# Where the matmul inputs of a transformer layer lie in on-chip memory, relative to their weights

## The chip, the core and the metric

The kernel runs on one core of a Trainium2 chip. The metric is the device time of one execution in microseconds (us), lower is better. A core has five engines that run their own instruction streams in order: PE (TensorE, matmuls, with its weight loads PEld), DVE (VectorE), ACT (ScalarE), POOL (GpSimd) and SP (SyncE, which here issues the DMA transfers). They meet through semaphores. Operands of a matmul lie in SBUF, the on-chip memory of 128 partitions; an address below is a byte offset within a partition. Results go to PSUM.

## The reference

One layer over 512 latent tokens and 256 context tokens of width 1024, all in float32. What matters:

```python
hx = modulate(rms_norm(x), sh1, sc1);  hc = modulate(rms_norm(ctx), csh1, csc1)
ak, av, qkv, db, da, aq, z, gate = split_cols(hx @ w_in)      # the context: the first five only
attn = latent_attention(q, keys of context and latents, values)    # 8 heads of 128
gdn  = gated DeltaNet, both directions, 8 heads, chunks: per chunk a unit triangular solve
       (I + strict(beta * dec * k k^T)) against [beta v, beta exp(gam) k], then a scan over chunks
       with dec = exp(gam_i - gam_j) masked to the triangle
y = sigmoid(g_a) * (attn @ w_pa) + sigmoid(g_d) * (gdn_out @ w_pd)
x = x + g1 * (y @ w_out)
h2 = modulate(rms_norm(x), sh2, sc2)
u = dwconv3(h2 @ w_up) + b;  a = silu(u_gate) * u_val          # d_ff = 2816
x = x + g2 * (a @ w_down);  return rms_norm(x, final_norm_w)
```

## The kernel before, in words

Every large float32 product is made of three matmuls in the type fp32r. The operands are split into a high part and a remainder, hi and lo, and `mm3` multiplies hi weights by hi inputs, hi weights by lo inputs, and lo weights by hi inputs into one PSUM bank. For weights, `load_w` does it: a DMA brings 128 x 1024 numbers into `wraw` (two buffers), ACT copies them into `whi`, DVE subtracts into `wlo` (three buffers each). The inputs are split once: `hxH`/`hxL` (latents), `hcH`/`hcL` (context), `atH`/`atL` (attention output), `g_s`, `g_n`, `g_k` (the gated DeltaNet output, in tiles that reuse the solver's memory), `yH`/`yL` (into the output projection), `h2H`/`h2L` (into the MLP) and `aH`/`aL` (the MLP's middle, into its down projection). A matmul mostly has 128 x 128 weights and a moving operand of 128 x 512.

The stages follow each other in this order: modulation and norms; the projection into pq; attention, woven with the convolutions' projections; then four pairs of DeltaNet heads, p = 0 to 3, woven with the remaining projections of hx; the two branch projections w_pa and w_pd; the output projection (into mc); the MLP up (mc) and down (mc); the last norm.

For a pair of heads `gdn_prep` (L874) loads `kT`, and for both directions the cumulated decays from the DRAM tile `gamdr`, broadcast to all partitions, into `NN` and `Gb`. It adds a triangular mask from `cst` and takes six exponentials on ACT for each, then adds `Gb` to `NN`. `Gb` has one buffer, which both heads of a pair use in turn. `gdn_solve` (L902) multiplies `NN` by the products kT x kT from the PSUM tile `pk`, and then runs the triangular solve of 32 x 32 blocks: tiles `C`, `X`, `R`, `prod`, on DVE for pair 0, on POOL for pairs 1 to 3. It ends in the transposed results `o_tr` and `o_nt`. `gdn_inv` (L943) assembles the inverse: POOL copies `o_tr` and `o_nt` into `TTm`, ACT into `Tm`, PE multiplies small blocks into `pb`, ACT copies them into `Y`, and so on. `gdn_scan` (L1011) walks the chunks. It needs four decay masks a pair, made by `decay_mask` (L1019): four broadcast transfers from `gamdr` each, two adds on POOL, four exponentials on ACT. They are the tiles `M2` in the code and `M` in the rows.

Inside the stages spoken of here PE keeps the order of the program. The other engines don't: a scheduler that runs a simulated timeline puts their instructions in order, by the priorities that the code sets (`first`, `sooner`, `solver`, `early`) and by when operands and memory are ready on that timeline. So the position of a mask's transfer on SP follows from the plan, and a change of tiles can move it.

Tiles are placed by pools on a left and a right stack of SBUF. `ws` holds wraw, whi and wlo; whi and wlo start at 448 modulo 512 bytes. In the last two stages the weights come from another pool, at 32 modulo 512. `cp` is the bottom of the left stack.

Of the kernel before, what the change touches and what calls it, by code (L numbers as in the profile page):

```python
# [78 lines left out]
def hybrid_layer_body(tc, x, ctxt, xT, consts, cols, rows, w_mod1, w_mod2, w_db, w_aq, w_cm, w_pa, w_pd, w_out,  # L79
# [54 lines left out]
    with es:  # L134
# [16 lines left out]
        def early():  # L151
            return tc.high_priority(offset=1000000)

        cst = cp.tile([P, C_TRI], F32, name="cst")
        with sooner():
            SP.dma_start(cst[:, 0:C_MS], consts[:, 0:C_MS])
        ident = cst[:, C_ID:C_ID + 128]
        ones = cst[:, C_ONE:C_ONE + 128]
        msk_s = (cst[:, C_MS:C_MS + 128], cst[:, C_MS + 128:C_MS + 256])
        msk_i = (cst[:, C_MI:C_MI + 128], cst[:, C_MI + 128:C_MI + 256])  # L160
        col = cp.tile([P, S_END], F32, name="col")
        with sooner():
            SP.dma_start(col, cols)
        for o in (8, 32):
            ts(col[:, S_BMOD + o:S_BMOD + o + 8], col[:, S_BMOD + o:S_BMOD + o + 8], 1.0, ALU.add)
        mhalf = cp.tile([P, 32], F32, name="mhalf")
        V.memset(mhalf, -0.5)
        mod = cp.tile([P, 48], F32, name="mod")
        modc = cp.tile([P, 16], F32, name="modc")
        csl = cp.tile([P, KT], F32, name="csl")  # L170

        def rsqrt(out, a, s, eps):
            n = a.shape[1]
            ts(out, a, s, ALU.mult, eps, ALU.add)
            tt(out, out, mhalf[:, 0:n], ALU.pow, G)

        def transpose(out, in_):
            T.transpose(out, in_, ident)
# [36 lines left out]
        szd = [dp.tile([P, NL], F32, name=f"szd{i}") for i in range(NH)]  # L215
        atd = [dp.tile([P, NL], F32, name=f"atd{i}") for i in range(NH)]

        beta = cp.tile([P, 96], F32, name="beta")
        gam = cp.tile([P, 96], F32, name="gam")
        ngam = cp.tile([P, 96], F32, name="ngam")  # L220
        eg = cp.tile([P, 96], F32, name="eg")
        kdec = cp.tile([P, 96], F32, name="kdec")
        hks = [cp.tile([P, 6], F32, name=f"hk{i}") for i in range(NH)]
        glast = cp.tile([P, 96], F32, name="glast")
        qsc = [cp.tile([P, 8], F32, name=f"qsc{i}") for i in range(4)]
        rkk = [cp.tile([P, 6], F32, name=f"rkk{i}") for i in range(NH)]
# [645 lines left out]
        rqh = lambda p, hh: rkq[2 * p + hh]  # L872

        def gdn_prep(p, eng=G):  # L874
            kT = gq.tile([P, 2, NA], F32, name="kT", tag="kT", bufs=2)
            for hh in range(2):
                SP.dma_start(kT[:, hh, :], kTd[2 * p + hh])
            g = gq.tile([P, 32], F32, name="g", tag="g", bufs=2)
            gT = gq.tile([P, 32], F32, name="gT", tag="gT", bufs=2)
            V.memset(g[:, 24:32], 0.0)  # L880
            for d in range(2):
                for hh in range(2):
                    r0 = d * 48 + (2 * p + hh) * 6
                    u = slice(12 * d + 6 * hh, 12 * d + 6 * hh + 6)
                    stt(g[:, u], beta[:, r0:r0 + 6], -1.0, rkk[2 * p + hh], ALU.mult, ALU.mult)
                    tt(g[:, u], g[:, u], rkk[2 * p + hh], ALU.mult)
            V.transpose(gT, g)
            NN = gq.tile([P, 12, P], F32, name="NN", tag="NN", bufs=2)
            for hh in range(2):
                u = slice(6 * hh, 6 * hh + 6)  # L890
                Gb = gq.tile([P, 6, P], F32, name="Gb", tag="Gb", bufs=1)
                for d, D in ((0, NN[:, u, :]), (1, Gb)):
                    r0 = d * 48 + p * 12 + hh * 6
                    SP.dma_start(D.rearrange("p a b -> p (a b)"),
                                 gamdr[r0:r0 + 6, :].rearrange("a b -> (a b)").partition_broadcast(P))
                    tt(D, D, msk_s[d].unsqueeze(1).to_broadcast([P, 6, P]), ALU.add, eng)
                    for c in range(6):
                        act(D[:, c, :], D[:, c, :], AF.Exp, scale=-1.0, bias=gam[:, r0 + c:r0 + c + 1])
                tt(NN[:, u, :], NN[:, u, :], Gb, ALU.add, eng)
            return [kT, gT, NN]  # L900

        def gdn_solve(pre, eng):  # L902
# [9 lines left out]
                        tt(NN[:, u, :], NN[:, u, :], pb[:, 0:n, :], ALU.mult)  # L912
                    yield
            with solver():
                q4 = lambda nm: gq.tile([P, 32, 32], F32, name=nm, tag="q4", bufs=3)
                C = q4("C")
                for b in range(4):
                    sb = slice(32 * b, 32 * b + 32)
                    V.transpose(C[sb, :, 12:24].rearrange("p j u -> p u j"), NN[sb, :, sb])
                    act(C[sb, :, 0:12], NN[sb, :, sb].rearrange("p u j -> p j u"))  # L920
                G.memset(C[:, :, 24:32], 0.0)
                X = q4("X")
                V.transpose(flat(X), flat(C))
                tt(X, X, gT.unsqueeze(2).to_broadcast([P, 32, 32]), ALU.mult)
                R = q4("R")
                G.memset(R, 0.0)
                G.memset(flat(R)[:, 0:1024:33], 1.0)
                if True:
                    for j in range(31):
                        m, n = 31 - j, j + 1  # L930
                        prod = gq.tile([P, 272], F32, name="prod", tag="prod")
                        pv = prod[:, 0:m * n].rearrange("p (i k) -> p i k", k=n)
                        tt(pv, X[:, j, j + 1:32].unsqueeze(2).to_broadcast([P, m, n]),
                           R[:, j:j + 1, 0:n].to_broadcast([P, m, n]), ALU.mult, eng)
                        tt(R[:, j + 1:32, 0:n], R[:, j + 1:32, 0:n], pv, ALU.add, eng)
                tt(R, R, gT.unsqueeze(2).to_broadcast([P, 32, 32]), ALU.mult)
                o_tr = q4("o_tr")
                V.transpose(o_tr.rearrange("p u s -> p s u"), R)
                o_nt = q4("o_nt")
                V.transpose(o_nt.rearrange("p u s -> p s u"), R.rearrange("p i k -> p k i"))  # L940
# [211 lines left out]
        def gsplit(h):  # L1152
            if h % 2 == 0:
                if h < 4:
                    ts_ = [gq.tile([P, 32, 32], F32R, name="g_s", tag="q4", bufs=3) for _ in range(2 if h == 0 else 1)]
                    if h == 2:
                        ts_.append(gq.tile([P, 12, P], F32R, name="g_n", tag="NN", bufs=2))
                elif h == 4:
                    ts_ = [gq.tile([P, 12, P], F32R, name="g_n", tag="NN", bufs=2),
                           gq.tile([P, 2, NA], F32R, name="g_k", tag="kT", bufs=2)]  # L1160
                else:
                    ts_ = [gq.tile([P, 2, NA], F32R, name="g_k", tag="kT", bufs=2)]
                    ls = [gpool[0].tile([P, 2, 2, P], F32R, name="g_m", tag="M2", bufs=4) for _ in range(2)]
                    ls = [l.rearrange("p a b c -> p (a b c)") for l in ls]
                ts_ = [flat(t) for t in ts_]
# [22 lines left out]
        def filler():  # L1188
# [43 lines left out]
                finish_pa(c, pa)  # L1232
            pas_es.close()
            yp = y_es.enter_context(tc.tile_pool(name="yp", bufs=1, side="right", reuse_waits="tile"))
            yt.append(yp.tile([P, KT, NL], F32R, align_bytes=2048, name="yH"))
            yt.append(yp.tile([P, KT, NL], F32R, align_bytes=2048, name="yL"))

            def finish_pd(c, pd):
                yH, yL = yt
# [93 lines left out]
        with ExitStack() as fe:  # L1333
# [2 lines left out]
            half = lambda i: slice(i * HT, i * HT + HT)  # L1336
            acc = [fs.tile([P, HT], F32, name=f"acc{i}") for i in range(2)]
            h2p = fe.enter_context(tc.tile_pool(name="h2p", bufs=1, reuse_waits="tile"))
            h2H = h2p.tile([P, KT, NL], F32R, align_bytes=2048, name="h2H")
            h2L = h2p.tile([P, KT, NL], F32R, align_bytes=2048, name="h2L")  # L1340

            def add_sq(c, i):
                sq = fs.tile([P, HT], F32, name="sq", tag="sq", bufs=2)
# [61 lines left out]
            oe.close()  # L1405
            y_es.close()
            fp = fe.enter_context(tc.tile_pool(name="fp", bufs=1, side="right", reuse_waits="tile"))
            aH = fp.tile([P, NFF, NL], F32R, align_bytes=2048, name="aH")
            aL = fp.tile([P, NFF, NL], F32R, align_bytes=2048, name="aL")
            ups = [h * NFF + j for j in range(NFF) for h in range(2)]  # L1410
            banks = {}

# [171 lines left out]
```

## Time and profile before

| what | value |
|---|---|
| time, median of 3 runs | 1303.81 us (1303.12 to 1305.67) |
| profiled execution: time, span | 1306.96 us, 1304.3 us |
| granted clock of PE, mean | 0.978 |
| PE busy, weight loads busy | 94%, 79% |
| DVE, ACT, POOL busy | 65%, 48%, 24% |
| DMA queue q1, share of 16 engines | 39.4% |

The profile is of one execution, with times from the start of its span. A row of the timeline gives start, duration, engine, line and operation, with the output and inputs, and in brackets the idle time of that engine ahead of it and what ended it. A row of the chain of waits gives start, duration and what was on the path that ended last; "SPq" is SP issuing a transfer. A group of instructions gives the shape, the count, the total busy time, the mean duration in ns, and the idle time in front. The matmuls are pipelined, so their durations overlap, and the distance between the starts of two neighbours is what PE spends on one.

### The profile page before, as it was taken

The numbers are of one execution on the slowest core, as the hardware profiler recorded it, in microseconds if no ns is written. First come the engines' busy times: TensorE is split into PE (matmuls) and PEld (weight loads), VectorE is DVE, ScalarE is ACT, GpSimd is POOL, SyncE is SP. The second block draws the span as 40 slices with busy tenths as digits, with TensorE's granted clock in tenths as the row PEclk, the third lists the DMA queues.
The fourth block names the chain that finished last, engine by engine and source line by source line (L and its number), as shares of the span: only waits on it lengthen the run. The fifth ranks groups of instructions, "written<-read, shape, count | busy, mean of one in ns | idle before, by whom it ended". The sixth has DMA issues, their size and how long they took to land.

```text
span 1304.3 us, 20850 instructions
## 1 busy us (share of the span) xinstructions
PE 1229.6 (94%) x7835; PEld 1031.3 (79%) x7835; DVE 848.4 (65%) x1625; ACT 626.3 (48%) x1403; POOL 308.3 (24%) x364
## 2 busy tenths in 40 slices
PE   7899999999968999899998999999999999999997
PEld 4487878999857877778787878788988888888886
DVE  5886987777759986685665556555576666663323
ACT  5453656666576665474453443233354444443221
POOL 1752420000143249559447300000000000000000
PEclk8999999999998999899999999999999999999998
DMA  8656631121373342543533555265043222233331
GB/s 321 227 169 197 223 118 62 65 86 50 111 252 105 124 140 91 177 131 110 178 120 116 170 165 168 92 219 190 9 129 97 97 97 95 91 94 97 90 100 65
DMA packets 70789, 170.80 MB, mean 131 GB/s; under 512 B 7872, under 2 KB 18720, under 8 KB 69280
## 3 DMA queue, kind: packets, MB, share of 16 engines
q1 hardware_dynamic: 70688, 169.47, 39.4%
q8 instruction: 61, 1.00, 0.3%
q14 instruction: 40, 0.33, 0.1%
HBM read 144.23 MB, written 25.21 MB: 130 GB/s over the span
## 4 chain that ended last, share of the span: by engine, by line
PE 66%; POOL 10%; DVE 9%; DMA 5%; ACT 4%; issue 3%; SPq 0%; POOLq 0%; DVEq 0%; ACTq 0%
PE mc L87 32%; PE mb L87 17%; PE pq L87 4%; POOL R L108 4%; POOL prod L108 4%; PE pb L87 3%; PE pS L87 3%; PE ab L87 2%; PE ab L91 1%; DMA Gb<-gamdr 1%; PE xb L91 1%; DVE wlo L108 1%; PE pk L87 1%; DMA sz<-gdr 1%; POOL NN L108 1%
## 5 line engine op out<-in xcount | busy, mean ns | idle before, releaser
L108 DVE TENSOR_TENSOR wlo<-wraw,whi 128x1024 fp32r<-128x1024 f32 x152 | 187.6, 1235 | 162.6 <-ACT whi L120 161.6
L120 ACT ACTIVATE whi<-wraw 128x1024 fp32r<-128x1024 f32 x152 | 159.1, 1048 | 205.5 <-PE mc L87 106.5
L87 PE MATMUL mb<-hxH,whi 128*128 128x512 f32 x384 | 165.1, 430 | 2.1 <-DVE R L108 1.9
L87 PE MATMUL mb<-hxL,whi 128*128 128x512 f32 x384 | 155.0, 404 | 0.0
L87 PE MATMUL mb<-hxH,wlo 128*128 128x512 f32 x384 | 154.3, 402 | 0.0
L87 PE MATMUL mc<-h2L,whi 128*128 128x512 f32 (+1 forms) x376 | 142.7, 379 | 0.0
L87 PE MATMUL mc<-h2H,whi 128*128 128x512 f32 (+1 forms) x376 | 142.3, 378 | 0.3 <-ACT whi L120 0.3
L87 PE MATMUL mc<-h2H,wlo 128*128 128x512 f32 (+1 forms) x376 | 140.8, 374 | 0.5 <-DVE wlo L108 0.5
L108 POOL TENSOR_TENSOR rc<-rc,mhalf 128x2 f32<-128x2 f32 x4 | 3.3, 818 | 459.4 <-DVE rc L114 459.4
L87 PEld LDWEIGHTS mb<-hxH,wlo 128*128 128x128 f32 x384 | 74.0, 193 | 18.3
L87 PEld LDWEIGHTS mb<-hxH,whi 128*128 128x128 f32 x384 | 74.6, 194 | 13.9 <-ACT t L120 2.1
L87 PEld LDWEIGHTS mb<-hxL,whi 128*128 128x128 f32 x384 | 74.6, 194 | 10.3
L87 PEld LDWEIGHTS mc<-h2H,whi 128*128 128x128 f32 x376 | 70.6, 188 | 14.9 <-ACT whi L120 0.5
L87 PEld LDWEIGHTS mc<-h2H,wlo 128*128 128x128 f32 x376 | 70.6, 188 | 14.7 <-DVE wlo L108 1.0
L87 PEld LDWEIGHTS mc<-h2L,whi 128*128 128x128 f32 x376 | 70.7, 188 | 12.2
L87 PE MATMUL mc<-aH,whi 128*128 128x512 f32 (+1 forms) x198 | 72.9, 368 | 0.6 <-DVE x L117 0.6
L87 PE MATMUL mc<-aL,whi 128*128 128x512 f32 (+1 forms) x198 | 73.0, 369 | 0.0
L87 PE MATMUL mc<-aH,wlo 128*128 128x512 f32 (+1 forms) x198 | 72.0, 364 | 0.0
L117 DVE SCALAR_TENSOR_TENSOR u<-mc,col,u 128x511 f32<-128x511 f32 x88 | 65.3, 746 | 1.4
L108 POOL TENSOR_TENSOR prod<-X,R 128x31 f32<-128x31 f32 (+15 forms) x93 | 53.5, 576 | 22.3 <-DVE X L108 15.4
L108 POOL TENSOR_TENSOR R<-R,prod 128x31 f32<-128x31 f32 (+15 forms) x93 | 57.1, 613 | 6.8
L87 PE MATMUL pq<-whi,hxH 128*128 128x256 f32 x192 | 56.6, 295 | 0.0
(354 smaller groups left out, 3078.3 us busy)
## 6 DMA issues: line engine op xcount, KB each, us to landing
wraw<-in_w_cm_dram SPq DMA_DIRECT2D x48, 512.0 KB, 3.9
wraw<-in_w_up_dram SPq DMA_DIRECT2D x44, 512.0 KB, 3.7
wmd<-in_w_mod_dram SPq DMA_DIRECT2D x64, 256.0 KB, 3.8
wm<-in_w_mod_dram SPq DMA_DIRECT2D x8, 1024.0 KB, 8.2
wraw<-in_w_down_dram SPq DMA_DIRECT2D x16, 512.0 KB, 3.5
wraw<-in_w_aq_dram SPq DMA_DIRECT2D x12, 512.0 KB, 4.8
M<-gamdr SPq DMA_DIRECT2D x64, 64.0 KB, 4.4
wraw<-in_w_pa_dram SPq DMA_DIRECT2D x8, 512.0 KB, 4.0
```

The costliest lines, as they stand in the source:

```text
L87: i = nc.tensor.matmul(*a, **k)
L91: i = nc.tensor.transpose(*a, **k)
L108: (eng or V).tensor_tensor(out=out, in0=a, in1=b, op=op)
L117: V.scalar_tensor_tensor(out=out, in0=a, scalar=s, in1=b, op0=op0, op1=op1)
L120: A.activation(out, a, f, **kw)
```

## The change

It changes where tiles lie, and computes the same. Small tiles that are read often or seldom (`cst`, `mod`, `beta`, `gam`, `hk0`) move from the left pool `cp` to a new right pool `cr`, and `col` gets 120 unused numbers, so that what lies above them shifts. The solver's tiles and kT and NN start at multiples of 2048 bytes. The hi and lo tiles of y, h2 and a become one tile each, with hi and lo behind each other and a shift of 64, 192 or 256 bytes from its start.

```diff
-        cst = cp.tile([P, C_TRI], F32, name="cst")
+        cr = es.enter_context(tc.tile_pool(name="cr", bufs=1, side="right"))
+        cst = cr.tile([P, C_TRI], F32, name="cst")
...
-        col = cp.tile([P, S_END], F32, name="col")
+        col = cp.tile([P, S_END + 120], F32, name="col")[:, 0:S_END]
...
-        mod = cp.tile([P, 48], F32, name="mod")
+        mod = cr.tile([P, 48], F32, name="mod")
...
+        def two(pool, k, by, name):
+            t = pool.tile([P, 2 * k * NL + 128], F32R, align_bytes=2048, name=name)
+            return [t[:, by // 4 + i * k * NL:by // 4 + (i + 1) * k * NL].rearrange("p (k n) -> p k n", n=NL) for i in range(2)]
...
-        beta = cp.tile([P, 96], F32, name="beta")
-        gam = cp.tile([P, 96], F32, name="gam")
+        beta = cr.tile([P, 96], F32, name="beta")
+        gam = cr.tile([P, 96], F32, name="gam")
...
-        hks = [cp.tile([P, 6], F32, name=f"hk{i}") for i in range(NH)]
+        hks = [(cp if i else cr).tile([P, 6], F32, name=f"hk{i}") for i in range(NH)]
...
-            kT = gq.tile([P, 2, NA], F32, name="kT", tag="kT", bufs=2)
+            kT = gq.tile([P, 2, NA], F32, name="kT", align_bytes=2048, tag="kT", bufs=2)
...
-            NN = gq.tile([P, 12, P], F32, name="NN", tag="NN", bufs=2)
+            NN = gq.tile([P, 12, P], F32, name="NN", align_bytes=2048, tag="NN", bufs=2)
...
-                q4 = lambda nm: gq.tile([P, 32, 32], F32, name=nm, tag="q4", bufs=3)
+                q4 = lambda nm: gq.tile([P, 32, 32], F32, name=nm, align_bytes=2048, tag="q4", bufs=3)
...
-            yt.append(yp.tile([P, KT, NL], F32R, align_bytes=2048, name="yH"))
-            yt.append(yp.tile([P, KT, NL], F32R, align_bytes=2048, name="yL"))
+            yt.extend(two(yp, KT, 64, "y2"))
...
-            h2H = h2p.tile([P, KT, NL], F32R, align_bytes=2048, name="h2H")
-            h2L = h2p.tile([P, KT, NL], F32R, align_bytes=2048, name="h2L")
+            h2H, h2L = two(h2p, KT, 192, "h2")
...
-            aH = fp.tile([P, NFF, NL], F32R, align_bytes=2048, name="aH")
-            aL = fp.tile([P, NFF, NL], F32R, align_bytes=2048, name="aL")
+            aH, aL = two(fp, NFF, 256, "a2")
```

The tiles g_s, g_n and g_k of `gsplit`, which reuse the memory of q4, NN and kT, get `align_bytes=2048` too.

By the addresses of the two builds, the distance from the weights to the input (start of the input minus start of the weights, modulo 512) is:

| input | before | after |
|---|---|---|
| hx | 32 | 64 |
| hc | 480 (-32) | 0 |
| at | 64 | 64 |
| g_s, g_n, g_k | 32 | 64 |
| y | 64 | 128 |
| h2 | 64 | 256 |
| a | 64 | 320 |

The order of PE is the same in both. On SP, ACT and POOL pair 0's decay masks change place. SP's transfers around pair 0's preparation, before (ktok and vtok are the scan's loads, ktd and vtd are stores of the convolutions):

```order
L894 DMA NN<-gamdr 128x768 x2
L1006 DMA vtok<-vtd_129 128x768
L1007 DMA ktok<-ktd_121 128x768
L1006 DMA vtok<-vtd_130 128x768
L305 DMA ktd_126<-co 128x768
L1007 DMA ktok<-ktd_122 128x768
L1023 DMA M_5591<-gamdr 128x128 x4
L1023 DMA M_5602<-gamdr 128x128 x3
L197 DMA wraw<-in_w_cm_dram 128x1024
L1023 DMA M_5602<-gamdr 128x128
L1023 DMA M_5613<-gamdr 128x128 x3
L894 DMA Gb<-gamdr 128x768
```

And after, from the same place on:

```order
L899 DMA NN<-gamdr 128x768 x2
L310 DMA ktd_129<-co 128x768
L202 DMA wraw<-in_w_cm_dram 128x1024
L899 DMA Gb<-gamdr 128x768 x2
L310 DMA vtd_136<-co 128x768
L202 DMA wraw<-in_w_cm_dram 128x1024
L899 DMA Gb<-gamdr 128x768
```

The scan's loads and the masks no longer stand ahead of Gb. They stand further down on SP, after:

```order
L1012 DMA ktok<-ktd_125 128x768
L1028 DMA M_5594<-gamdr 128x128
L310 DMA vtd_138<-co 128x768
L202 DMA wraw<-in_w_cm_dram 128x1024
L1028 DMA M_5594<-gamdr 128x128 x3
L1028 DMA M_5605<-gamdr 128x128 x4
L1028 DMA M_5616<-gamdr 128x128 x3
L202 DMA wraw<-in_w_cm_dram 128x1024
L1028 DMA M_5616<-gamdr 128x128
L1028 DMA M_5627<-gamdr 128x128 x4
L343 DMA qTd_116<-co 128x512
L1013 DMA qT<-qTd_116 128x512
```

The two wraw loads between them are the ones that go out at 436.78 us and behind it in the trace before. On POOL, before, the masks' adds precede the adds of Gb:

```order
L108 TENSOR_TENSOR NN<-NN,cst 128x768 x2
L108 TENSOR_TENSOR M_5591<-M_5591,cst 128x256 x2
L108 TENSOR_TENSOR M_5602<-M_5602,cst 128x256 x2
L108 TENSOR_TENSOR M_5613<-M_5613,cst 128x256 x2
L108 TENSOR_TENSOR M_5624<-M_5624,cst 128x256 x2
L108 TENSOR_TENSOR Gb<-Gb,cst 128x768
```

After, they stand directly ahead of the copies into TTm that open pair 0's inverse:

```order
L108 TENSOR_TENSOR Gb<-Gb,cst 128x768
L108 TENSOR_TENSOR rkk_180<-rkk_180,mhalf 128x6
L108 TENSOR_TENSOR rkk_181<-rkk_181,mhalf 128x6
L108 TENSOR_TENSOR M_5594<-M_5594,cst 128x256 x2
L108 TENSOR_TENSOR M_5605<-M_5605,cst 128x256 x2
L108 TENSOR_TENSOR M_5616<-M_5616,cst 128x256 x2
L108 TENSOR_TENSOR M_5627<-M_5627,cst 128x256 x2
L966 COPY TTm<-o_tr 32x12x32 x4
L966 COPY TTm<-o_nt 32x12x32 x4
```

On ACT the sixteen exponentials of the masks move the same way, from in front of Gb's exponentials to in front of the copies into Tm.

More of the change, by code (lines that the diff above doesn't have):

```diff
@@ L1154, in gsplit @@
                 if h < 4:
-                    ts_ = [gq.tile([P, 32, 32], F32R, name="g_s", tag="q4", bufs=3) for _ in range(2 if h == 0 else 1)]
+                    ts_ = [gq.tile([P, 32, 32], F32R, name="g_s", align_bytes=2048, tag="q4", bufs=3) for _ in range(2 if h == 0 else 1)]
                     if h == 2:
-                        ts_.append(gq.tile([P, 12, P], F32R, name="g_n", tag="NN", bufs=2))
+                        ts_.append(gq.tile([P, 12, P], F32R, name="g_n", align_bytes=2048, tag="NN", bufs=2))
                 elif h == 4:
-                    ts_ = [gq.tile([P, 12, P], F32R, name="g_n", tag="NN", bufs=2),
-                           gq.tile([P, 2, NA], F32R, name="g_k", tag="kT", bufs=2)]
+                    ts_ = [gq.tile([P, 12, P], F32R, name="g_n", align_bytes=2048, tag="NN", bufs=2),
+                           gq.tile([P, 2, NA], F32R, name="g_k", align_bytes=2048, tag="kT", bufs=2)]
                 else:
-                    ts_ = [gq.tile([P, 2, NA], F32R, name="g_k", tag="kT", bufs=2)]
+                    ts_ = [gq.tile([P, 2, NA], F32R, name="g_k", align_bytes=2048, tag="kT", bufs=2)]
                     ls = [gpool[0].tile([P, 2, 2, P], F32R, name="g_m", tag="M2", bufs=4) for _ in range(2)]
```

## The prediction

> **What bounds the kernel now.** I read the page from the top: busy time, then the shares of the chain that ended last.
>
> ```profile
> span 1304.3 us, 20850 instructions
> PE 1229.6 (94%) x7835; PEld 1031.3 (79%) x7835; DVE 848.4 (65%) x1625; ACT 626.3 (48%) x1403; POOL 308.3 (24%) x364
> PE 66%; POOL 10%; DVE 9%; DMA 5%; ACT 4%; issue 3%; SPq 0%; POOLq 0%; DVEq 0%; ACTq 0%
> PE mc L87 32%; PE mb L87 17%; PE pq L87 4%; POOL R L108 4%; POOL prod L108 4%; PE pb L87 3%; PE pS L87 3%; PE ab L87 2%; PE ab L91 1%; DMA Gb<-gamdr 1%; PE xb L91 1%; DVE wlo L108 1%; PE pk L87 1%; DMA sz<-gdr 1%; POOL NN L108 1%
> ```
>
> PE's matmuls are two thirds of the chain, and half of the kernel's time is matmuls into mc and mb. So two things can pay: a smaller step from one matmul to the next, or the removal of a place where PE stands still. The other 34% lies with POOL, DVE, DMA and ACT, mostly in the middle, where the recurrence's solver runs; there a faster matmul buys nothing.
>
> I then asked for PE's timeline and the chain around 380 us, where the chain leaves PE and runs through a transfer.
>
> ```profile
> 380.90 0.40 PE L87 MATMUL mb<-hxH,wlo 128*128 128x512 f32 x1
> 390.06 1.22 PE L87 MATMUL pk<-kT 128*128 128x128 f32 x4 [8.76 <-DVE NN L108]
> ...
> 376.37 0.38 SPq L894
> 376.79 7.33 DMA M<-gamdr
> 384.18 0.73 POOL M L108
> 385.83 1.55 ACT Gb L120 x5
> 389.32 0.69 DVE NN L108
> ```
>
> The first two rows are PE: it stands still for 8.76 us until DVE has multiplied NN. The five behind are the chain: the transfers of the decay masks M come first, then POOL's add, then ACT's exponentials of Gb, which stand on ACT behind those of M, then NN. Pair 0's solver waits for masks that only its scan, much later in the program, reads.
>
> **The change, part by part: the order.** The merged and moved tiles leave PE's order as it is. On SP, ACT and POOL the sixteen mask transfers, eight adds and sixteen exponentials of pair 0 go behind the preparation of pairs 0 and 1. What held Gb back shows on SP and DVE.
>
> ```profile
> 367.14 6.33 SPq L1023 DMA_DIRECT2D M<-gamdr  x7
> 374.42 1.85 SPq L1023 DMA_DIRECT2D M<-gamdr  x4
> 370.13 0.94 DVE L108 TENSOR_TENSOR NN<-NN,Gb 128x768 f32<-128x768 f32 x1
> 381.39 0.96 DVE L108 TENSOR_TENSOR Gb<-Gb,cst 128x768 f32<-128x768 f32 x1 [0.62 <-DMA Gb<-gamdr]
> 385.54 1.84 ACT L120 ACTIVATE Gb<-Gb,gam 128x128 f32<-128x128 f32 x6
> DMA to landing us min/median/max: 3.4/4.4/7.1
> ```
>
> Gb's buffer is free when DVE's NN add ends at 370.13 + 0.94 = 371.07. Its transfer is issued at 376.37, since eleven mask issues stand ahead of it. The last row is tile Gb: 4.4 us to landing. Without the masks ahead: issue 371.1, landing 375.5, DVE's add 376.5, six exponentials 378.4, the second NN add (0.95) 379.4, the multiply (0.69) 380.1, and PE goes on at about 380.9, where it now runs out of matmuls. Of the 8.76 us some 8.0 go. Bounds: all 8.76, or 3 us less if the landing takes 7.1 instead of 4.4.
>
> This work isn't gone. It comes back just before pair 0's inverse, in front of POOL's copies into TTm and ACT's copies into Tm.
>
> ```profile
> 436.78 5.56 SPq L197 DMA_DIRECT2D wraw<-in_w_cm_dram  x2
> 439.65 1.07 ACT L120 ACTIVATE whi<-wraw 128x1024 fp32r<-128x1024 f32 x1 [1.11 <-PE mb L87]
> 449.82 2.15 POOL L961 COPY TTm<-o_tr 32x384 f32<-32x384 f32 x4 [20.24 <-DVE o_tr L938]
> 452.01 3.06 POOL L961 COPY TTm<-o_nt 32x384 f32<-32x384 f32 x4
> 449.72 1.06 ACT L120 ACTIVATE Tm<-o_tr 32x384 f32<-32x384 f32 x2 [1.01 <-DVE o_tr L938]
> 453.82 0.97 ACT L120 ACTIVATE Y<-pb 32x384 f32<-32x384 f32 x2
> 456.77 0.21 PE L87 MATMUL pb<-Y,o_nt 32*32 32x32 f32 x1
> L120 ACT ACTIVATE M<-M,ngam x64: 385/390/406, 377.6 to 752.1; 128x128 f32<-128x128 f32 x64
> L108 POOL TENSOR_TENSOR M<-M,cst x32: 721/732/1735, 374.7 to 750.1; 128x256 f32<-128x256 f32 x32
> ```
>
> POOL is idle for 20.24 us ahead of the copies, which covers eight adds of 0.73 us (5.9 us), if the masks have landed. In the new order eleven of the sixteen transfers stand ahead of the second of the two wraw loads of the first row and five behind it. Everything up to there moves with the removed gap, so I use the old clock: the second wraw goes out by 442.3, the five masks behind it by 442.3 + 5 x 0.46 (1.85 / 4) = 444.6, landing at 449.0 with 4.4 us and 451.7 with 7.1. POOL's last add then ends at 449.7 to 452.4, and its copies start 0 to 2.6 us late. On ACT two exponentials behind that add move Tm from 449.72 to 450.4 or 453.1; Y ends at 454.8 and PE needs it at 456.77, so 2 us are covered. Queued behind POOL's copies are pair 1's solver and the preparation of pair 2, behind ACT's Tm the Y that PE waits for. Loss 0 to 3 us; I take 2, nearer the upper end, because sixteen masks in a string land later than a single Gb. The order is worth -8 + 2 = -6 us.
>
> **The change, part by part: the offsets.** Let d be the start of the moving tile minus that of the weights, in bytes modulo 512. By the two layouts hx and the gated outputs g go from 32 to 64, at stays at 64, y goes from 64 to 128, h2 from 64 to 256 and a from 64 to 320. I took unbroken runs of 512-wide matmuls at full granted clock from PE's timeline and divided the time between two starts by the matmuls between.
>
> ```profile
> 354.69 0.39 PE L87 MATMUL mb<-hxH,whi 128*128 128x512 f32 x1
> 358.18 0.39 PE L87 MATMUL mb<-hxH,whi 128*128 128x512 f32 x1
> ...
> 763.03 0.40 PE L87 MATMUL mb<-atL,whi 128*128 128x512 f32 x1
> 767.39 0.39 PE L87 MATMUL mb<-atH,wlo 128*128 128x512 f32 x1
> ...
> 999.74 0.39 PE L87 MATMUL mc<-h2L,whi 128*128 128x512 f32 x1
> 1003.86 0.39 PE L87 MATMUL mc<-h2L,whi 128*128 128x512 f32 x1
> ```
>
> hx: 3.49 / 15 = 232.7 ns; at: 4.36 / 19 = 229.5 ns; h2: 4.12 / 18 = 228.9 ns. So d = 32 costs 3.8 ns a matmul over d = 64. The groups by shape and the chain say how many matmuls that concerns.
>
> ```profile
> L87 PE MATMUL mb<-hxL,whi 128*128 128x512 f32 x384 | 155.0, 404 | 0.0
> L87 PE MATMUL mb<-hcL,whi 128*128 128x256 f32 x112 | 31.5, 281 | 0.0
> L87 PE MATMUL ab<-PH,VL 128*128 128x256 f32 x96 | 27.0, 281 | 0.0
> ...
> 842.63 36.56 PE mb L87 x149
> 944.92 338.57 PE mc L87 x1510
> ...
> 472.00:537.00 65.00, 18.98 (x48) 9.08 (x48) 0.00 (x0) 0.00 (x0) 0.99 0.37 119
> 570.00:632.00 62.00, 18.99 (x48) 8.96 (x48) 0.00 (x0) 0.00 (x0) 0.99 0.37 118
> ```
>
> hx has 3 x 384 = 1152 matmuls, 4.4 us at 3.8 ns if all lay on the path. They don't. In the two stretches of the last rows (hxL alone, one of three) 2 x 3 x 48 = 288 matmuls take 67 us of 127, PE waits for the solver, and a faster matmul only lengthens that wait. The page's chain has mb at 17% of 1304.3 = 222 us, of which 36.6 belong to g at the end (842.63); the 185 left hold at most 185 / 0.2327 = 795 matmuls of this kind, hc's and at's among them. Two thirds of that, 530 x 3.8 ns, is 2.0 us; bounds 0 and 3.0. g lies wholly on the chain there: 149 x 3.8 = 0.6 us, bounds 0 and 0.6 by the same two rows.
>
> The 256-wide matmuls of hc go from d = -32 to 0. Their mean of 281 ns equals that of PH on VL, which stands at d = 128: I cost them at nothing. The same goes for the 256-wide parts of y, h2 and a. Bounds for all of these: 336 (3 x 112) matmuls by the 3.8 ns above either way, 1.3 us.
>
> y, h2 and a leave a distance that already runs at 228.9 ns for 128, 256 and 320, which no 512-wide row of this trace shows with full weights. The row at 944.92 us holds 1510 of h2's and a's back to back. A loss like that of d = 32 would give 1510 x 3.8 = 5.7 us slower. If they gain as much again, 5.7 us faster. I take nothing: d = 64 stands at the lower of the two steps seen, and nothing shows a third.
>
> A rule of the Trainium skill speaks against any gain from offsets. TensorE: Matmul & The Clock Gate, section "Step-by-step: what each phase is for", says that PE has two independent read ports on SBUF, one for the streamed operand and one for the weights, so that their addresses should not meet. By it the offset terms would be 0 and the sum -6.0. The 232.7 against 228.9 ns of the same shape on this trace differ, so I don't follow it in full.
>
> **The sum.** Order -6.0, hx -2.0, g -0.6, hc 0, y, h2 and a 0: -8.6 us. The profiled execution's span would go from 1304.3 to 1295.7. That execution took 1306.96 us in all, 2.7 beyond its span and 3.15 above the median of the runs shown, 1303.81. Taken off the median: 1295.2, rounded up to **1296**, since the gap can only be shortened by what lands on time.
>
> **The rivals.**
> (1) The new distances of y, h2 and a are better still. For it: the tail is 338.57 us of pure matmul chain. Against it: at d = 64 PE already shows its lowest step. 1296 - 5.7 is 1290.
> (2) Operand addresses don't matter, and hx is slower than h2 for another reason (other engines busy, PSUM being read meanwhile). For it: one run of each was measured, in different stages. Against it: the run of at (763 us) lies in the same part of the program as those of hx and still steps at 229.5. Only the order counts: 1303.8 - 6.0 = 1298. This is also where the Trainium skill's two read ports, cited above, would end.
> (3) The late masks take the gap's place. For it: the slow landing of 7.1 us stands on this very stretch. If Gb lands in 7.1, the gap gives only 5.0; if the last mask comes 2 us after my late case, the copies start 4.6 late; with 1.4 of the offsets: 1303.8 - 5.0 + 4.6 - 1.4 = 1302. Against it: both have to be late at once.
> (4) Slower: the mask transfers don't move with the gap. Before, eleven issues and a landing took from 367.14 to 376.79 + 7.33 = 384.12, 17 us. If all sixteen go out only behind the second wraw, at 442.3 by the absolute clock, and need 17 us again, the last lands at 459.3, POOL's add ends at 460.0, its copies 5.2 us later at 465.2 instead of 455.1. That is 10.1 us late for all that POOL does next, and 8.8 for PE by ACT's Tm. The removed gap is then swallowed whole: 1303.8 + 10.1 - 2.6 for hx and g = 1311. It decides from a last landing after about 454. Against it: eleven of the sixteen stand ahead of that wraw in the new order.
>
> **How the numbers follow.** My forecast (1293 to 1299) 0.42; rival 1 0.17; rival 2 0.15; rival 3 0.13; rival 4 0.13. Faster holds the forecast, 1 and 2, 0.74; rival 3 is "same", 0.13; rival 4 slower, 0.13. Within 0.2% is 2.6 us, about what a measurement of this kernel tells from no change. For 8 in 10 the range takes rival 1 below, with a us beyond, and ends at rival 3 above: 1288 to 1303.
>
> **What would show it.** In the changed profile PE's wait for NN before pk near 381 should be under 1.5 us, and no M issue should stand ahead of Gb on SP. POOL's copies into TTm should start with at most 3 us more wait than the solver sets. Steps of hx and g should read 229 ns; those of h2, a and y 229. Wrong would be: h2 or a at another step than 229 by more than 2 ns (5 us then come from the tail), hx still at 232.7, or a wait of PE behind Y or Tm between 440 and 470 as long as the gap that went.

## The result, and the profile after

The changed kernel takes 1297.36 us (median of five runs, 1296.49 to 1299.34), the kernel before 1305.09 us beside it (1303.12 to 1305.70). The ratio is 0.9947, 95% interval 0.9931 to 0.9963: 0.5% faster. The forecast was 1296, 7.8 us less than before; the medians differ by 7.7.

One sentence on the kernel above needs a correction: only the 256-wide tail of the output projection takes its weights from the pool at 32 modulo 512; the MLP's weights, up and down, start at 448. The table of distances holds as it stands for all 512-wide matmuls.

The page of the changed kernel, its span, busy times and shares of the chain:

```profile
span 1296.9 us, 20854 instructions
PE 1219.5 (94%) x7835; PEld 1026.6 (79%) x7835; DVE 847.1 (65%) x1625; ACT 625.4 (48%) x1403; POOL 308.1 (24%) x364
PE 64%; DVE 11%; POOL 10%; DMA 5%; issue 3%; ACT 2%; SPq 0%; POOLq 0%; DVEq 0%; ACTq 0%
```

PE is 10 us less busy. DVE has 11% of the chain instead of 9, ACT 2 instead of 4. Here is the place of the gap, from the timelines of SP, DVE and PE:

```profile
371.90 9.26 SPq L899 DMA_DIRECT2D Gb<-gamdr  x2
375.46 0.96 DVE L108 TENSOR_TENSOR Gb<-Gb,cst 128x768 f32<-128x768 f32 x1 [2.73 <-DMA Gb<-gamdr]
379.86 0.95 DVE L108 TENSOR_TENSOR NN<-NN,Gb 128x768 f32<-128x768 f32 x1
382.60 0.71 PE L87 MATMUL pk<-kT 128*128 128x128 f32 x4 [0.60 <-DVE NN L108]
```

Gb goes out at 371.90, when DVE's first NN add has ended (370.93 + 0.95), and not at 376.37. PE waits 0.60 us instead of 8.76. Since PE runs the same matmuls in the same order in both, its starts can be set against each other one by one: at this place the changed kernel gains 8.2 us.

The gap had a second price. The rows are stretches of both traces with the granted clock (the first three before, the last after; behind the engines stand the clock, the DMA share and GB/s):

```profile
376.00:381.00 5.00, 4.92 (x35) 4.07 (x33) 2.65 (x4) 4.57 (x14) 3.30 (x4) 1.00 0.71 226
381.00:390.00 9.00, 0.29 (x2) 0.00 (x0) 3.87 (x5) 5.04 (x15) 2.11 (x3) 0.76 0.45 152
390.00:396.00 6.00, 5.95 (x16) 4.88 (x17) 4.50 (x6) 4.17 (x6) 2.88 (x3) 0.51 0.15 44
...
373.00:377.50 4.50, 4.50 (x28) 4.50 (x27) 2.00 (x3) 2.84 (x11) 0.00 (x0) 0.62 0.32 83
```

After the idle stretch PE's clock was granted at 0.51 for 6 us, which is some 2.9 us of matmul work lost. The changed kernel has a slow stretch here too, of 4.5 us at 0.62 (1.7 us lost), behind a shorter pause of PE. So the clock costs the changed kernel about a microsecond less here. Against that, PE waits 1.1 us longer for co. The rows give total, number and longest wait, from 355 to 430 us before and over the same matmuls, 354 to 420.5 us, after:

```profile
PE xb L91 <- DVE co L117: 5.1, 3, 2.8
...
PE xb L91 <- DVE co L117: 6.2, 3, 3.5
```

By PE's starts the changed kernel is 1.5 us ahead before this place (at 360 us) and 9.6 us ahead after it (at 430 us), so the place as a whole gives 8.1.

Not all of it stays. At the start of pair 0's inverse PE stands still in the changed kernel (the DVE row is the transposition that it waits for), and before the last matmuls on g it waits longer (chain rows of before and of after):

```profile
443.20 1.97 DVE L945 STREAM_TRANSPOSE o_nt<-R 128x1024 f32<-128x1024 f32 x1
445.22 0.22 PE L87 MATMUL pb<-o_nt,NN 32*32 32x32 f32 x1 [1.58 <-DVE gT L892]
...
837.70 2.61 DMA sz<-szd
...
829.82 4.65 DMA sz<-szd
```

The transposition ends at 445.17; gT, which the bracket names, is a small one right behind it. What the inverse costs PE shows between two of its matmuls around it, the same two in the kernel before, the changed one and, for later, the changed one without the masks' adds:

```profile
444.09 0.39 PE L87 MATMUL mb<-hxH,wlo 128*128 128x512 f32 x1
460.14 0.40 PE L87 MATMUL mb<-hxH,wlo 128*128 128x512 f32 x1
...
434.46 0.39 PE L87 MATMUL mb<-hxH,wlo 128*128 128x512 f32 x1
454.79 0.39 PE L87 MATMUL mb<-hxH,wlo 128*128 128x512 f32 x1
...
433.28 0.39 PE L87 MATMUL mb<-hxH,wlo 128*128 128x512 f32 x1
450.08 0.39 PE L87 MATMUL mb<-hxH,wlo 128*128 128x512 f32 x1
```

They lie 16.05 us apart before, and 20.33 in the changed kernel: of the 8.1 us, 4.3 are lost again. Two waits make 2.0 of them (0.45 and 1.58); behind the waits the clock is granted at 0.57 from 445 to 449 us, where it is 1.00 before (452 to 456).

The transfer of sz took 2 us longer than in the other trace; in the traces of all the other kernels with one buffer for sz that row is 2.4 to 3.6 us. The tail, finally, the MLP's wide matmuls and ahead of them the 425 that hold the output projection and the MLP's 256-wide part, as the chain counts them (before: 63.34 and 338.57):

```profile
879.19 63.34 PE mc L87 x425
...
873.38 63.80 PE mc L87 x425
939.58 336.42 PE mc L87 x1510
```

The MLP gains 2.15 us, where nothing was forecast; the piece with the output projection loses 0.46.

### The profile page after: what moved, and what is told of

The parts are those of the page before. It is cut to its first block, busy times and chain, and to the rows that moved or that the text cites. A ratio compares the mean times of both kernels' runs of the same rounds, so it can differ in the third digit from the quotient of the medians.

```text
span 1296.9 us, 20854 instructions
## 1 busy us (share of the span) xinstructions
PE 1219.5 (94%) x7835; PEld 1026.6 (79%) x7835; DVE 847.1 (65%) x1625; ACT 625.4 (48%) x1403; POOL 308.1 (24%) x364
## 4 chain that ended last, share of the span: by engine, by line
PE 64%; DVE 11%; POOL 10%; DMA 5%; issue 3%; ACT 2%; SPq 0%; POOLq 0%; DVEq 0%; ACTq 0%
PE mc L87 32%; PE mb L87 17%; POOL R L108 4%; POOL prod L108 4%; PE pb L87 4%; PE pS L87 3%; PE ab L87 2%; PE pq L87 2%; DMA Gb<-gamdr 2%; PE ab L91 1%; DVE wlo L108 1%; PE pk L87 1%; PE xb L91 1%; DMA wmd<-in_w_mod_dram 1%; DVE macc L377 1%
## 5 line engine op out<-in xcount | busy, mean ns | idle before, releaser
L87 PE MATMUL mc<-h,whi 128*128 128x512 f32 (+1 forms) x752 | 219.7, 376 | 0.3 <-ACT whi L120 0.3
L87 PEld LDWEIGHTS mc<-h,whi 128*128 128x128 f32 x752 | 138.0, 188 | 25.9 <-ACT whi L120 0.5
L87 PE MATMUL mb<-hxL,whi 128*128 128x512 f32 x384 | 152.0, 396 | 0.0
L87 PE MATMUL mc<-h,wlo 128*128 128x512 f32 (+1 forms) x376 | 141.3, 376 | 0.5 <-DVE wlo L108 0.5
L87 PE MATMUL mc<-a,whi 128*128 128x512 f32 (+1 forms) x396 | 111.4, 367 | 0.6 <-DVE x L117 0.6
L87 PEld LDWEIGHTS mc<-a,whi 128*128 128x128 f32 x396 | 71.3, 188 | 13.1 <-DVE x L117 0.8
L87 PEld LDWEIGHTS mc<-h,wlo 128*128 128x128 f32 x376 | 70.8, 188 | 13.8 <-DVE wlo L108 1.0
L87 PE MATMUL mc<-a,wlo 128*128 128x512 f32 (+1 forms) x198 | 72.7, 367 | 0.0
L87 PE MATMUL pq<-whi,hxH 128*128 128x256 f32 x192 | 55.3, 288 | 0.0
L87 PE MATMUL pq<-wlo,hxH 128*128 128x256 f32 x192 | 53.5, 279 | 0.2 <-DVE wlo L108 0.2
L87 PE MATMUL pq<-whi,hxL 128*128 128x256 f32 x192 | 53.3, 278 | 0.0
```

The lines of the kernel that those rows point to most:

```text
L87: i = nc.tensor.matmul(*a, **k)
```

## The experiments

Each was timed against the kernel before on the same chip, with the differences below worked out from the ratio of the two and 1305 us; where one execution alone was timed, there is no interval.

**The three parts apart.** The change is a sum of three edits that can be made one at a time. Only the alignment:

```diff
-            kT = gq.tile([P, 2, NA], F32, name="kT", tag="kT", bufs=2)
+            kT = gq.tile([P, 2, NA], F32, name="kT", align_bytes=2048, tag="kT", bufs=2)
...
# the same for NN, the solver's tiles, g_s, g_n, g_k
```

> Only the alignment to 2048 bytes of kT, NN, the solver's tiles and g; hx stays at 32, y, h2 and a at 64. It moves the masks on SP, ACT and POOL as the whole change does. My theory: PE's wait for NN before pk falls from 8.8 us to under 1, the late masks give 2 to 3 us back, g's step falls by 3 to 4 ns: 5 to 7 us faster than before, most of the whole change's 7.7. Rival, that the offsets of the big inputs carry the gain: at most 2 us faster.

Measured: 1300.73 us, ratio 0.9975 (0.9959 to 0.9990), 3.3 us faster (1.3 to 5.4): less than the 5 to 7 that I expected, more than the rival's 2. The gap is gone and the masks stand late.

Only the small tiles in the right pool and the padding behind col:

```diff
-        cst = cp.tile([P, C_TRI], F32, name="cst")
+        cst = cr.tile([P, C_TRI], F32, name="cst")
...
-        col = cp.tile([P, S_END], F32, name="col")
+        col = cp.tile([P, S_END + 120], F32, name="col")[:, 0:S_END]
...
# mod, beta, gam and hk0 go to cr too
```

> Only the small tiles moved to the right pool and col padded: hx goes from 32 to 64, hc from -32 to 0, the masks stay where they were. My theory: hx's step falls from 232.7 to about 229.5 ns and the time by about 2 us (0 to 3). Rival, two independent read ports: step and time unchanged (within 1 us).

Measured: 1301.64 us, ratio 0.9975 (0.9962 to 0.9987), 3.3 us faster (1.7 to 5.0). hx's step fell from 233.3 to 230.0 ns, in the mean over neighbours that nothing parts (steps above 260 ns left out).

Only y, h2 and a in merged tiles:

```diff
-            h2H = h2p.tile([P, KT, NL], F32R, align_bytes=2048, name="h2H")
-            h2L = h2p.tile([P, KT, NL], F32R, align_bytes=2048, name="h2L")
+            h2H, h2L = two(h2p, KT, 192, "h2")
...
# the same for y (64) and a (256)
```

> Only y, h2 and a in merged tiles at 128, 256 and 320; hx and order as before. By the steps of the changed kernel's trace: h2 226.8 instead of 228.9 ns over 984 wide matmuls, -2.1 us, y 232.3 instead of 228.9 over 120, +0.4 us, a unchanged: 1.7 us faster. My forecast on record for this part was 0; the rival with better distances for all had 5.7 us; two independent read ports: 0 and no step changed.

Measured: 1303.88 us, ratio 0.9991 (0.9977 to 1.0005): 1.2 us faster, not clear of no change. In its trace the MLP up gains 2.0 us at an even pace of 0.39 us in each 40, as 984 matmuls at 2.1 ns less give.

The three sum to 7.7 us, the whole to 6.9 by its ratio. PE's wait for NN, as each trace's list of waits has it (total, number, longest; first the alignment, then the moved tiles, then the merged tiles):

```profile
PE pk L87 <- DVE NN L108: 0.6, 1, 0.6
...
PE pk L87 <- DVE NN L108: 10.5, 2, 10.4
...
PE pk L87 <- DVE NN L108: 9.9, 1, 9.9
```

So the order comes with the alignment alone, and the other two parts gain while they keep the gap.

**Is it the order, or the aligned addresses?** A second buffer for Gb, with no alignment:

```diff
-                Gb = gq.tile([P, 6, P], F32, name="Gb", tag="Gb", bufs=1)
+                Gb = gq.tile([P, 6, P], F32, name="Gb", tag="Gb", bufs=2)
```

> The kernel before with a second buffer for Gb, no alignment, all distances as before. The masks then also stand late on SP, ACT and POOL. My theory: the 8.8 us were Gb's transfer behind the masks, so PE's wait for NN before pk falls under 1 us, and the time by 3 to 6 us as with the alignment alone (without the 0.6 of g). Rival, that aligned addresses of the solver's tiles made the gain: no change from before.

Measured: 1301.78 us, ratio 0.9984 (0.9972 to 0.9996), 2.1 us faster (0.5 to 3.7). PE's matmuls into pk no longer wait for NN:

```profile
L87 PE MATMUL pk<-kT 128*128 128x128 f32 x96 | 16.2, 311 | 0.2
```

The gap closes without any alignment, so it was Gb's transfer behind the masks. The gain is no larger than the alignment's, and under the 3 to 6 that I expected: by either way the order is worth 2 to 3 us, half of the 6.0 that I forecast. The traces show where the rest goes. Between the matmuls at 360 and 430 us of the trace before, the alignment alone gains 7.6 us and the second buffer 8.0; between those at 444 and 460, around pair 0's inverse, they lose 3.7 and 7.7. With the right pool alone, or the merged tiles alone, which keep the old order of the masks, the second stretch changes by 0.1 us at most.

**What do the late masks cost?** The changed kernel without the eight adds on POOL that mask pair 0's decays (its scan then computes with unmasked decays):

```diff
+                    if p:
-                    tt(M2[:, d], M2[:, d], msk_i[d].unsqueeze(1).to_broadcast([P, 2, P]), ALU.add, G)
+                        tt(M2[:, d], M2[:, d], msk_i[d].unsqueeze(1).to_broadcast([P, 2, P]), ALU.add, G)
```

> The changed kernel without the eight adds on POOL that put the triangle into pair 0's decay masks, so pair 0's scan uses unmasked decays and its numbers are other ones. If the late masks cost time by POOL's adds running beside DVE's solver: the two slow wlo subtractions on DVE (7.8 us for five instead of 6.1) are gone, o_nt ends 1.5 to 2 us earlier and the time falls by 1 to 3 us. If the late masks cost nothing and PE waits there only because DVE's solver is now the longer chain: within 1 us of the changed kernel.

Measured: 1292.76 us, ratio to before 0.9915 (0.9900 to 0.9929), so some 4.2 us faster than the changed kernel, more than the 1 to 3 expected. In the trace the two matmuls around pair 0's inverse, shown above, lie 16.80 us apart, against 20.33 in the changed kernel and 16.05 in the one before: 3.5 of the 4.3 us are back, 2.0 of them the waits and the rest the slow clock behind them, which this execution hasn't got. That lead is lost again by 650 us of this one execution, in part to longer stretches of slow clock near 530 and 622 us, and before g's last matmuls it gains 2.3 us by a short transfer of sz. So the trace shows what the adds cost at the inverse; how much of the timed 4.2 us is theirs it doesn't show. POOL's timeline in the changed kernel shows that the masks are not what its copies wait for:

```profile
440.30 1.54 POOL L108 TENSOR_TENSOR M<-M,cst 128x256 f32<-128x256 f32 x1 [0.36 <-DMA M<-gamdr]
443.48 3.21 POOL L966 COPY TTm<-o_tr 32x384 f32<-32x384 f32 x4 [1.64 <-DVE o_tr L943]
```

The last add ends at 441.84, and POOL then waits 1.64 us more for o_tr. It is o_tr that is late. Two steps of pair 0's solver on DVE, in the changed kernel (where POOL adds masks from 431.94 on) and without the adds:

```profile
435.01 0.71 DVE L108 TENSOR_TENSOR prod<-X,R 128x135 f32<-128x135 f32 x1
435.76 0.70 DVE L108 TENSOR_TENSOR R<-R,prod 128x135 f32<-128x135 f32 x1
...
433.27 0.30 DVE L108 TENSOR_TENSOR prod<-X,R 128x135 f32<-128x135 f32 x1
433.61 0.30 DVE L108 TENSOR_TENSOR R<-R,prod 128x135 f32<-128x135 f32 x1
```

And the solver's ends, its first transposition and that into o_tr, in the kernel before, the changed one, and the one without the adds:

```profile
447.58 2.10 DVE L938 STREAM_TRANSPOSE o_tr<-R 128x1024 f32<-128x1024 f32 x1
...
383.82 3.60 DVE L924 STREAM_TRANSPOSE C<-NN 32x384 f32<-32x384 f32 x4
441.28 2.06 DVE L943 STREAM_TRANSPOSE o_tr<-R 128x1024 f32<-128x1024 f32 x1
...
382.55 3.61 DVE L924 STREAM_TRANSPOSE C<-NN 32x384 f32<-32x384 f32 x4
437.83 2.10 DVE L943 STREAM_TRANSPOSE o_tr<-R 128x1024 f32<-128x1024 f32 x1
```

From C to o_tr: 55.8 us before (C at 391.77), 57.5 in the changed kernel, 55.3 without the adds. While POOL adds, many of DVE's two-input operations take longer (from 430 us on the solver's own take 2.2 us more in all than without the adds), and DVE's solver is the longest chain there. The masks' transfers and ACT's exponentials are still there without the adds, so they are not the cause. The wlo subtractions that I had named in the expectation were not it: their mean stayed at 1.55 us without the adds. The Trainium skill, SBUF — State Buffer, section "Who interferes with whom", says that a DVE instruction with two SBUF inputs contends with a GpSimd instruction that reads SBUF; the 0.70 against 0.30 us agree.

**Which distances are slow?** One kernel with all eight slices of h2, and all 22 of a, at different distances:

```diff
...
+            n = NL + (16 if k == KT else 8)
+            t = pool.tile([P, 2 * k * n], F32R, align_bytes=2048, name=name)
...
```

> The changed kernel with h2's eight slices at 64, 128, ... 448, 0 (64 bytes further per slice) and a's 22 slices 32 bytes apart from 64 on, so that one run shows the step at every distance. If the distance modulo 512 sets the step: 64 about 229, 128 about 232, 256 about 227, 320 about 229, 32 about 233, and h2's table agrees with a's at the same distance. If addresses don't matter: all slices within 1 ns. If it isn't the distance but something about a tile (its place, its neighbour), the two tables disagree.

One execution: 1302.22 us. Each slice's triple repeats its value to 0.1 ns in nearly all of the 41 passes, but it isn't the value of that distance alone. h2's step was 230.0 ns at 0 and at 256, 232.7 at 64 and 320, 232.3 at 128 and 384, 231.7 at 192 and 448: a period of 256, with every slice slower than in a run at one distance of 64 or 256, since the neighbour slices have others. a's hi and lo slices came to lie 192 apart there, so its values can't be read as one distance's. As a table of distances this failed; what it gave was the period. So I held each stage at one distance:

```diff
-            h2H, h2L = two(h2p, KT, 192, "h2")
-            aH, aL = two(fp, NFF, 256, "a2")
+            h2H, h2L = two(h2p, KT, 448, "h2")
+            aH, aL = two(fp, NFF, 128, "a2")
# y: 32; in the second kernel h2 64, a 32, y 96
```

> The changed kernel with h2 held at distance 0, a at 192 and y at 96. If the step depends on the distance modulo 256 and odd multiples of 32 are the slow ones (32 gave 233.4): h2 226.7 as at 256, y at 96 about 233, a at 192 between 229 and 232. If it isn't periodic: h2 at 0 away from 226.7 by more than 1 ns.

> The changed kernel with h2 held at distance 128, a at 96 and y at 160. By the distance alone: h2 as y did at 128, 232.3 ns, so the tail is 984 x 5.6 ns = 5.5 us longer than the changed kernel's; a and y at odd multiples of 32 about 233 (a: 462 x 4.3 = 2.0 us longer). If the stage and not the distance set y's 232.3: h2 at 128 stays under 229.

One execution each: 1299.60 and 1304.26 us. From PE's timeline, first and last row of unbroken runs: h2 at 256 (the changed kernel, 108 matmuls), at 0 (108), and at 128 (108); a at 320 (the changed kernel, 129) and at 192 (126).

```profile
985.25 0.39 PE L87 MATMUL mc<-h,wlo 128*128 128x512 f32 x1
1009.73 0.39 PE L87 MATMUL mc<-h,wlo 128*128 128x512 f32 x1
...
984.98 0.39 PE L87 MATMUL mc<-h,wlo 128*128 128x512 f32 x1
1009.46 0.39 PE L87 MATMUL mc<-h,wlo 128*128 128x512 f32 x1
...
984.66 0.39 PE L87 MATMUL mc<-h,wlo 128*128 128x512 f32 x1
1009.86 0.39 PE L87 MATMUL mc<-h,wlo 128*128 128x512 f32 x1
...
1214.94 0.39 PE L87 MATMUL mc<-a,wlo 128*128 128x512 f32 x1
1244.47 0.39 PE L87 MATMUL mc<-a,wlo 128*128 128x512 f32 x1
...
1214.97 0.39 PE L87 MATMUL mc<-a,wlo 128*128 128x512 f32 x1
1244.37 0.39 PE L87 MATMUL mc<-a,wlo 128*128 128x512 f32 x1
```

24.48 / 108 = 226.7 ns, 226.7, 25.20 / 108 = 233.3; 29.53 / 129 = 228.9, 29.40 / 126 = 233.3. The steps found with one distance held:

| distance | 0 | 32 | 64 | 96 | 128 | 160 | 192 | 256 | 320 |
|---|---|---|---|---|---|---|---|---|---|
| ns a matmul | 226.7 | 233.3 | 228.9 | 233.3 | 232.3 to 233.3 | 234.3 | 233.3 | 226.7 | 228.9 |
| seen in | h2 | hx, g | y, h2, a | y, a | y, h2 | y | a | h2, a, y | a |

The MLP's chain in the second kernel, 1510 matmuls with h2 at 128 and a at 96:

```profile
936.26 345.12 PE mc L87 x1510
```

That is 8.7 us above the changed kernel's 336.42; 984 x 6.6 ns and 462 x 4.4 ns give 8.5. Where two of y, h2 and a share a distance, they agree to 1 ns. Not all came as expected: a at 192 is slower than the 229 to 232 that I gave it. And the distance isn't the whole rule. hx and at, whose matmuls are woven with other work, step at 229.9 to 230.4 ns at 64. At 64 too, g steps at 230 ns in the changed kernel, but at 232.4 in the second kernel here, where neither its tiles nor its order changed: behind a stall it settles on 233 to 234 instead of a cycle of 226, 229 and 232. The same distance can thus run in two patterns; what picks one stays open.

**All at 256.** Seventy-two unused numbers behind col put the weights at 256 and every large input at 0:

```diff
-        col = cp.tile([P, S_END + 120], F32, name="col")[:, 0:S_END]
+        col = cp.tile([P, S_END + 72], F32, name="col")[:, 0:S_END]
# and two(..., 0, ...) for y, h2 and a
```

> The changed kernel with 72 instead of 120 unused numbers behind col and no shift of y, h2 and a: whi and wlo then start at 256 and hx, at, g, y, h2 and a all at 0, distance 256 for all. If 256 is the best distance wherever it is held: every step about 227 ns; against the changed kernel y -0.6 us (5.5 x 120), a -1.0 (2.2 x 462), g and at -0.7, hx -1 to -3: 3 to 5 us faster than the changed kernel, about 1293. If 256 suits h2 alone (the kernel with eight distances gave 230.0 there): within 1 us of the changed kernel.

Measured: 1297.38 us, ratio to before 0.9943 (0.9925 to 0.9961): no different from the changed kernel, and not the 3 to 5 us faster that I expected. y, h2, a and g all step at 226.7 to 227.5, and the two tail pieces of its chain take 63.35 and 335.51 us, 1.36 less. But hx, the largest term of that expectation, steps at 229.6 ns, hardly less than the 230.3 at 64. And matmuls of 256 columns, which none of these tables holds, got slower. In the projection into pq, whi and wlo are the moving operand and hx the weights, at distance 480 before, 448 in the changed kernel and 256 here. First and last row of 22 steps, in the changed kernel and here:

```profile
132.69 0.29 PE L87 MATMUL pq<-whi,hxL 128*128 128x256 f32 x1
135.20 0.28 PE L87 MATMUL pq<-wlo,hxH 128*128 128x256 f32 x1
...
133.23 0.28 PE L87 MATMUL pq<-whi,hxL 128*128 128x256 f32 x1
135.87 0.29 PE L87 MATMUL pq<-wlo,hxH 128*128 128x256 f32 x1
```

2.51 / 22 = 114.1 ns and 2.64 / 22 = 120.0. In the mean over all neighbours at full clock it is 118.3 ns before, 114.8 in the changed kernel and 119.5 here; 576 matmuls at 4.7 ns are 2.7 us; by PE's starts 1.2 us are lost to the changed kernel between 100 and 175 us. The narrow matmuls of h2 and a read 119.6 to 119.9 at 0 and 256 as well, a's at 192 114.1: the distance that is best for 512 columns is among the slowest for 256. In the one profiled execution more is lost to the clock between 560 and 770 us (granted 0.96, against 0.98 in the changed kernel; by PE's starts some 2 us):

```profile
560.00:770.00 210.00, 195.80 (x1625) 166.68 (x1626) 125.32 (x248) 101.54 (x250) 112.14 (x170) 0.96 0.44 143
...
560.00:770.00 210.00, 196.31 (x1644) 166.83 (x1644) 125.02 (x250) 102.05 (x251) 111.86 (x170) 0.98 0.46 144
```

Whether that layout brings this clock about, or only this execution had it, stays open, and so does how the timed sum divides.

**The load of sz.** Among the last heads one tile sz is loaded only when the one before is used up. A second buffer in the kernel before, at both places that make such a tile:

```diff
-                sz = gpool[0].tile([P, NL], F32, name="sz", tag="sz", bufs=1)
+                sz = gpool[0].tile([P, NL], F32, name="sz", tag="sz", bufs=2)
```

> The kernel before with a second buffer for sz alone. The masks stand late here too, so the order's 2 to 4 us as with a second buffer for Gb come with it; the loads of sz for the last heads (2.6 us on the chain at 837.70) go out ahead: another 2.5 to 5 us. 1296 to 1299 if both hold; 1301.5 if sz is hidden anyway.

Measured: 1296.07 us, ratio 0.9930 (0.9915 to 0.9945), 9.1 us faster. This edit, too, moves the masks behind the preparation, so 2 to 3 us are the order's and some 6, by subtraction, those of sz; the trace shows 1.1 us gained on the kernel before near 800 us and 3.6 at g's last matmuls.

**Together.** The kernel before with the right pool, distance 256 for all large inputs, and second buffers for Gb and sz:

```diff
...
+        col = cp.tile([P, S_END + 72], F32, name="col")[:, 0:S_END]
...
+            gq.tile([P, 56], F32, name="gqpad")
...
+                Gb = gq.tile([P, 6, P], F32, name="Gb", tag="Gb", bufs=2)
+                sz = gpool[0].tile([P, NL], F32, name="sz", tag="sz", bufs=2)
```

> The kernel before with the small tiles in the right pool, 72 unused numbers behind col and 56 below the solver's tiles (distance 256 for all large inputs), two buffers for Gb and two for sz. Sum against before: second Gb -3 to -6, hx -3, y, h2, a, at and g at 256 about -4, sz loaded ahead for the last heads -2.6 to -4.6 (the transfer on the chain before and after): about 1291, 1288 to 1294. If the second sz buffer is swallowed by the scan: 1294.

Measured: 1289.39 us, ratio 0.9887 (0.9874 to 0.9901): 1.1% faster than before, and faster than the changed kernel, as the sum had it. (Its pq matmuls step at 119.5 ns too, so 256 for everything isn't the best there either.) The last transfer of sz is off its chain, as the lines of the stretch from 815 to 835 us show:

```profile
by line: PE mb L87 71.5%; PE pb L87 8.9%; ACT whi L120 5.3%; PE pb L91 4.4%; DVE sz L117 3.8%; DVE gd L117 3.5%; DVE g_m L108 3.0%; issue 0.8%
```

The same with pair 0's masks early:

```diff
-            masks = {c: decay_mask(c) for c in (4, 3, 5, 2)}
+            with early() if p == 0 else ExitStack():
+                masks = {c: decay_mask(c) for c in (4, 3, 5, 2)}
```

> The kernel with all distances at 256 and second buffers for Gb and sz, with pair 0's decay masks given the priority of the preparation, so that they come some 10 us earlier. If the masks' cost is POOL's adds beside DVE's solver, they still run beside it: within 1.5 us of the kernel without the priority (1289). If it is their late landing: 1 to 3 us faster.

Measured: 1291.21 us, ratio 0.9893 (0.9875 to 0.9912): no gain over 0.9887. But the edit moved less than meant: two of the eight adds run at 424 us, some 8 us earlier, the other six between 431 and 439 us as without it. All eight still run beside DVE's solver, and around the inverse the trace loses 2.4 us more. So this doesn't tell what masks that land well ahead would cost.

## Why the prediction was right, and where not

The time came out as forecast, but two of its terms were off, in opposite directions.

- **The gap.** Right in place, cause and size: 8.0 us forecast, 8.2 measured, and the second buffer for Gb closes it alone. Not foreseen were the slow clock behind it, about another 1 us, and longer waits for co, which take it back.
- **What the late masks cost.** I took 2 us, for POOL's copies and ACT's Tm waiting behind the masks. That step failed in its mechanism: POOL was done 1.6 us before its copies could start. The adds slow DVE's solver, which pair 0's inverse waits for, and the waits bring a slow clock with them: 4.3 us at the inverse in the changed kernel, 0.8 without the adds, 3.7 and 7.7 in the traces with the alignment and the second buffer alone. The price lies above the 0 to 3 that I gave. So the order is worth 2 to 3 us as timed, not 6.
- **hx.** The mechanism was right: the step fell from 233.3 to about 230 ns. Timed alone the edit gives 3.3 us (1.7 to 5.0) against 2.0 forecast. The sum leaves out the 576 narrow matmuls into pq, where hx is the weights: their step fell from 118.3 to 115.2 ns in that trace, which is up to 1.8 us. Its profiled execution lacks one stretch of half clock that the one before has near 123 us, so some of its 3 us there isn't the step's.
- **g.** The step fell from 233.3 to 230.2 ns (229.9 at full clock), close to the 229 forecast. The chain's stretch on g didn't show it, because a transfer of sz took 2 us longer in that execution. It was not timed apart.
- **y, h2 and a.** Taken at nothing, bounded at 5.7 us either way. h2 at 256 is 2.2 ns a matmul faster, y at 128 slower by 3.4, a at 320 the same: 1.7 us in the traces. The step that failed is "d = 64 stands at the lower of the two steps seen, and nothing shows a third". Rival 1 was right for h2 alone.
- **Addresses that can't meet.** Rival 2 gave 0 for all offsets. The Trainium skill, TensorE: Matmul & The Clock Gate, section "Step-by-step: what each phase is for", has the two operands' read ports independent; 226.7 against 233.3 ns for the same matmuls at another address differ from what follows from it, and the measurement decides.
- **Rivals 3 and 4** named the right work and the right place, but the wrong victim: POOL's copies waited for the solver, not for the masks.

Offsets together give about 4.5 us and the order 2 to 3, where I had 2.6 and 6.0: the sum was right by luck, because the errors cancel.

## What to carry to other kernels

When a scheduler plans the order, a change of tiles can be a change of order: alignment, a second buffer for Gb and a second buffer for sz each moved the same sixteen transfers. Compare the planned order first, and test the order apart from what the edit was meant to do. And when work moves to where an engine is idle, ask what runs beside it, not only what is queued behind it. A placement that suits one shape of matmul has to be measured on the others too.

## What the runs showed of the hardware

PE's step for 512-wide fp32r matmuls with fresh 128 x 128 weights each time depends on where the input starts relative to the weights: 226.7 ns at 0 or 256 bytes modulo 512, 228.9 at 64 or 320, 232 to 234 at the other multiples of 32 tried. For 256 columns the order is another: 119.5 to 119.9 ns at 0 or 256 in pq, h2 and a, 114.8 at 448 in pq and 114.1 at 192 in a. A mix of distances in one accumulation gives neither value, and g at 64 ran at 230 ns in one execution and at 232.4 in another. After a pause of 9 us PE ran at a granted clock of 0.51 for 6 us. Two-input operations on DVE took 0.70 us instead of 0.30 while POOL was adding in the same stretch.
